# Differential attention on one core: a context projection group moves to another PSUM bank, and in two units of nine the first third of a projection group moves ahead of values and transposes

## The chip, the core and the metric

The kernel runs on one core of a Trainium2 chip. The core has a TensorE for matrix products (PE in the profile, PEld for its weight loads), a VectorE (DVE), a ScalarE (ACT), a GpSimd (POOL) and a SyncE (SP), which issues this kernel's DMAs. Each engine works through its own list of instructions in order and waits on semaphores for the others. Products are written to PSUM, here a tile PS of eight banks with 512 float32 columns each on 128 partitions; only VectorE and ScalarE read it in this kernel.

The metric is the device time of one execution in microseconds. The time before is 2961.78 us, the median of three runs (2960.13 to 2971.89).

## The reference

A two-layer backbone over 1024 latent tokens and 256 context tokens of width 1024. Layer 0 mixes tokens by differential attention, layer 1 by an S5 state space model; both are followed by an MLP. The change lies in the attention of layer 0: eight heads, each with two query/key halves of 64 columns and values of 128.

```python
def attend(q, k, v):
    s = jnp.einsum('bqhcd,bkhcd->bhcqk', q, k).astype(jnp.float32)
    p = jax.nn.softmax(s, axis=-1)
    w = p[:, :, 0] - lam * p[:, :, 1]
    o = jnp.einsum('bhqk,bkhe->bqhe', w.astype(v.dtype), v)
    return rmsnorm(o, subln_g) * (1.0 - lambda_init)
...
k_all = jnp.concatenate([k_c, k_l], axis=1)
o_l = lax.map(lambda qq: attend(qq, k_all, v_all), qb)
...
o_c = attend(q_c, k_c, v_c)
```

Latent queries read all 1280 keys, context queries the 256 context keys.

## The kernel before

Products that need more precision than one pass gives are made as three: each operand is split into a high and a low part (`split`: ScalarE copies the high part, VectorE or GpSimd subtracts), and `mm3` adds high by high, high by low and low by high (lines 132 to 134, so three matmuls stand for one product of 128 rows).

`phase_b` is the attention. For each of eight heads h it goes through nine units u. Unit 0 holds the 256 context queries, units 1 to 8 hold 128 latent queries each. In a unit

- `scores` (L517) multiplies queries by keys. In units 1 to 8 it fills 2560 columns, which are banks 0 to 4 of PSUM: 1280 for each half. In unit 0 it uses half of each of banks 0 to 3; bank 4, the scores' fifth, is then unused.
- `maxima` (L538 for unit 0, L542 for the others) lets VectorE copy the negated scores out with their minimum, one instruction for each half, which frees the banks. `exps` (L549, L552) takes the exponentials on ScalarE, `combine` (L560 to L563) forms the weight difference on VectorE.
- `w_part` (L570, L575) transposes the weights of the unit before in three parts on TensorE, into bank 5, the upper half of bank 6, and bank 7 (or bank 5 again, when the unit has a projection group). `w_evac` empties them: the first part directly (L583 on ScalarE, L584 on VectorE), the others by a ScalarE copy (L588) that GpSimd splits (L589, L590). In units whose values belong to a latent pair, the flag `late` puts all of this behind the exponentials.
- `values` multiplies the transposed weights of a pair of units by the values, into bank 6: 6 matmuls in unit 2, 30 in units 1, 4, 6 and 8, none in units 0, 3, 5 and 7.
- `proj_group` projects part of the next head's keys (T=1) or queries (T=0) for one token group g: 2 is the context (256 columns), 0 and 1 are the latent halves (512 columns). The table AHEAD says which unit makes which:

```python
AHEAD = {0: ((1, 2), (1, 0)), 2: ((1, 1),), 3: ((0, 2),), 5: ((0, 0),), 7: ((0, 1),)}
```

A group is eight products, 24 matmuls, and a list of steps behind it. All groups take their bank from `self.qb`, which in `phase_b` holds bank 7 alone. A context group is evacuated by `direct` (L462 on ScalarE, L463 on VectorE) into the staging tile `stg` and stored to DRAM. A latent group goes through `evac` (L467, L468), a swap of rows by four DMAs, a product with the sine on GpSimd (L473), a sum on VectorE (L476), a split and a store. Unit 0 has two groups: the first is made whole before the scores, the second, like the single group of the other units, in three pieces (`fills`) behind the three parts of the transposes.

On PE, DVE, ACT and POOL the order of `phase_b` is the order in which it is written (`self.manual()`). SyncE's order, and everything outside `phase_b`, is set by a scheduler that plans with its own estimate of times. Key tiles, queries and values are loaded back from DRAM by `load_k`, `load_q` and `load_v`; `load_k(h + 1, 1)` is written in unit 8, since its buffer is that of a key tile which the scores of unit 8 read.

Of the kernel before, what the change touches and what calls it, by code (L numbers as in the profile page):

```python
# [70 lines left out]
class Prog:  # L71
# [64 lines left out]
    def split(self, hi, lo, src, lo_eng=None):  # L136
        self.nc.scalar.activation(hi, src, AF.Copy)  # L137
        (lo_eng or self.nc.vector).tensor_tensor(lo, src, hi.bitcast(F32), ALU.subtract)  # L138
# [302 lines left out]

        return split

    def proj_group(self, h, T, g, wt):

        nc = self.nc
        n, c0 = self.G_TOK[g], (256, 768, 0)[g]
        b = self.qb.next()[:, 0:n]
        scale = 1.0 if T else -0.125
        t = slice(c0 - 256, c0 + 256)  # L450
        hT = self.hT[g]
        q, sw, qc, s = self.rq, self.rs, self.rc, self.stg[:, :, 0:n]

        def product(k):
            return lambda: self.mm3(b, wt[k][0], wt[k][1], hT[0][:, k], hT[1][:, k], k == 0, k == 7)

        def out():
            dst = self.Kd if T else self.Qd
            self.dma(dst[h % 2, :, :, c0 : c0 + n].rearrange("l p n -> p l n"), s.bitcast(F32))

        def direct():
            nc.scalar.activation(s[:, 0], b, AF.Copy, scale=scale)  # L462
            nc.vector.scalar_tensor_tensor(s[:, 1], b, scale, s[:, 0].bitcast(F32), ALU.mult, ALU.subtract)  # L463
            out()

        def evac():
            nc.scalar.activation(q, b, AF.Copy, scale=scale)  # L467
            nc.vector.scalar_tensor_tensor(qc, b, scale, self.cosT[:, t], ALU.mult, ALU.mult)  # L468
            for j in range(4):
                self.dma(sw[32 * j : 32 * j + 32], q[32 * (j ^ 1) : 32 * (j ^ 1) + 32])  # L470

        def sine():
            nc.gpsimd.tensor_tensor(sw, sw, self.sinT[:, t], ALU.mult)  # L473

        def add():
            nc.vector.tensor_tensor(qc, qc, sw, ALU.add)  # L476

        def store():
            self.split(s[:, 0], s[:, 1], qc)
            out()  # L480

        return [product(k) for k in range(8)], [direct] if g == 2 else [evac, None, sine, add, store]
# [143 lines left out]
    def phase_b(self):  # L626
# [14 lines left out]
        def load_k(h, c):  # L641
            K = loaded[h, "k", c] = self.rv(0, 1280) if (h, c) == (7, 1) else Kr.next()
            for k0, k1 in ((0, 256), (256, 1280)):
                self.dma(K[:, k0:k1].bitcast(F32), self.Kd[h % 2, c, :, k0:k1])

        def load_v(h):
            V = loaded[h, "v"] = Vr.next(), Vr.next()
            for j in range(2):
                self.dma(V[j].bitcast(F32), self.Vd[h, j])

        def load_q(h, pair):
            Q = Qr.next()
            cols = slice(256 * pair, 256 * pair + 256)
            self.dma(Q.bitcast(F32), self.Qd[h % 2, :, :, cols].rearrange("l p n -> p l n"))
            loaded[h, pair] = Q

        def values(h, pair):
            V = loaded[h, "v"]
            last = 2 if pair == 0 else 10
            for kt in range(last):  # L660
                self.mm3(pb[:, 0:256], V[0][:, kt], V[1][:, kt], self.wT[0][:, kt], self.wT[1][:, kt],
                         kt == 0, kt == last - 1)
# [107 lines left out]
        def wo_group(i):  # L770
            g = 2 if i > 7 else i // 4
            c0 = 128 * (i - self.G_TILES[g][0])
            b = self.bank(i - 6 if 6 < i < 8 else 7)

            def product(k):
                hh, hl = (t[:, k, c0 : c0 + 128] for t in self.oT[g])
                return lambda: self.mm3(b, hh, hl, wt6[k][0], wt6[k][1], k == 0, k == 5)

            def out():
                wsum = wsums.next()  # L780
                nc.scalar.activation(wsum, b, AF.Copy)
                self.dma(self.wod[i], wsum)

            return [product(k) for k in range(6)], [out]
# [13 lines left out]
        wts = {1: split(1)}  # L798
# [12 lines left out]
        with self.manual():  # L811
            for n in range(72 + 5):
                h, u = units[n] if n < 72 else (8, 9)
                front = n < 72
                groups = []
# [7 lines left out]
                if front:  # L823
                    K = loaded[h, 'k', 0], loaded[h, 'k', 1]
                    pair = (u + 1) // 2
                    Q = loaded[h, pair]
                    s0 = hst[:, 0, h]
                    p, sn, sm = (p0.next(), p1), self.stat.next(), self.stat.next()
                    if u == 5 and h < 7:
                        load_v(h + 1)  # L830
                        load_k(h + 1, 0)
                    if u % 2 == 0 and u < 8 and (h, pair + 1) not in loaded:
                        load_q(h, pair + 1)
                    if h < 7:
                        groups = [self.proj_group(h + 1, *a, wts[a[0]]) for a in self.AHEAD.get(u, ())]
                    if len(groups) == 2:
                        for f in groups[0][0] + groups[0][1]:
                            f()
                    self.scores(u, Q, K)
                    if u == 8 and h < 7:  # L840
                        load_k(h + 1, 1)
                        load_q(h + 1, 0)
                        load_q(h + 1, 1)
                    self.maxima(u, p, sm)
# [6 lines left out]
                if 65 <= n < 75:  # L851
                    groups = [wo_group(wo_order[n - 65])]
                fills = [[], [], []]
                if h >= 7 and groups:
                    fills = [groups[0][0][i : i + 2] for i in (0, 2, 4)]
                elif groups:
                    fills = [groups[-1][0][i:j] for i, j in (((0, 4), (4, 8), (8, 8)) if u == 3 else ((0, 3), (3, 6), (6, 8)))]
                if pv:
                    values(*pv)
                for part in range(3):  # L860
# [1399 lines left out]
```

## Time and profile before

| | before |
|---|---|
| median of the runs | 2961.78 us |
| the profiled execution, its own time | 2967.23 us |
| its span, first to last instruction | 2965.4 us |
| granted TensorE clock over the span | 0.98 |
| attention, first scores of head 0 to the last of head 7 | 227.5 to about 891 us |
| busy in 400 to 500 us: PE, DVE, ACT, POOL | 93.4, 79.6, 56.2, 62.6 us of 100 |

The page has the span and the busy time of each engine, and names lines as `L517`. In an answer on waits, a line gives the engine and line that waited, after the arrow the one that ended the wait, the total in us, how often, and the longest. A row of the timeline gives start and duration in us, the engine, the line, the operation with output and inputs, the shape and a count; in brackets stand the idle time of that engine just before and who ended it. "SPq" is the issue of a DMA, whose transfer comes later. A row of windows gives the stretch, its length, the busy time of PE, PEld, DVE, ACT and POOL, the granted clock as a share of full speed, the share of the DMA engines' time, and GB/s.

### The profile page before, as it was taken

To read this page: it belongs to the slowest core of one execution; us is meant where nothing else is said; L and a number is where in the kernel's file an instruction comes from. 1 tells how busy PE (TensorE), PEld (TensorE's weight loads), DVE (VectorE), ACT (ScalarE), POOL (GpSimd) and SP (SyncE) were. 2 spreads that over 40 slices of the span, in tenths; PEclk is the share of its full clock that TensorE was granted. 3 is DMA by queue.
4 is the path that set the end of the run, shared out by engine and by line. 5 is a ranking of instruction groups with operands and counts; after the bars stand their busy time and mean duration, and the time that the engine had idled before them with its cause. 6 is when DMAs were issued, how large, how long until landed. Compare 5 with 4: busy or idle time off the path is not lost.

```text
span 2965.4 us, 44388 instructions
## 1 busy us (share of the span) xinstructions
PE 2795.9 (94%) x16040; PEld 2315.8 (78%) x16040; DVE 1884.1 (64%) x2777; ACT 1311.9 (44%) x2412; POOL 1010.5 (34%) x911
## 2 busy tenths in 40 slices
PE   6998999999899999999999999969899999999999
PEld 4686878778777787788777778768788778887887
DVE  6356787787764564444487863788733676658566
ACT  3324555555553753333422231347534655334443
POOL 2313576666653600000100000668401323326324
PEclk9999999999999999999999999989999999999999
DMA  9953344444634546422566673468944475467544
GB/s 277 301 188 132 126 154 146 154 144 133 203 124 149 156 127 193 141 94 89 177 189 189 182 232 109 134 193 269 302 134 150 148 228 195 152 201 267 162 137 140
DMA packets 422920, 512.95 MB, mean 173 GB/s; under 512 B 57142, under 2 KB 295980, under 8 KB 421548
## 3 DMA queue, kind: packets, MB, share of 16 engines
q1 hardware_dynamic: 422700, 510.11, 55.2%
q8 instruction: 126, 2.06, 0.3%
q14 instruction: 94, 0.77, 0.1%
HBM read 351.29 MB, written 154.50 MB: 171 GB/s over the span
## 4 chain that ended last, share of the span: by engine, by line
PE 49%; DVE 8%; DMA 5%; issue 5%; POOL 4%; ACT 3%; SPq 2%; DVEq 0%; POOLq 0%; ACTq 0%
PE PS L132 15%; PE PS L133 15%; PE PS L134 15%; SPq L80 2%; PE PS L1722 1%; PE PS L1763 1%; ACT F L552 1%; DVE F L542 1%; DVE FD L1742 1%; DVE H L138 1%; DMA K<-in_mlp_w 1%; PE PS L517 1%; DVE FD L1639 1%; DMA W<-in_mlp_w 1%; DMA H<-hidd 1%
## 5 line engine op out<-in xcount | busy, mean ns | idle before, releaser
L132 PE MATMUL PS<-H,R 128*128 128x512 f32 (+1 forms) x816 | 306.2, 378 | 23.2 <-ACT F L588 15.8
L132 PE MATMUL PS<-H 128*128 128x512 f32 x768 | 300.7, 393 | 2.9 <-ACT H L137 2.9
L134 PE MATMUL PS<-H 128*128 128x512 f32 x768 | 300.2, 392 | 1.9 <-DVE H L138 1.9
L133 PE MATMUL PS<-H 128*128 128x512 f32 x768 | 301.2, 392 | 0.0
L133 PE MATMUL PS<-H,R 128*128 128x512 f32 (+1 forms) x816 | 297.5, 365 | 1.4 <-POOL H L138 1.4
L134 PE MATMUL PS<-H,R 128*128 128x512 f32 (+1 forms) x816 | 297.0, 365 | 0.0
L137 ACT ACTIVATE R<-W 128x512 fp32r<-128x512 f32 (+1 forms) x186 | 132.9, 720 | 194.4 <-PE PS L133 149.5
L132 PE MATMUL PS<-R,H 128*128 128x512 f32 x540 | 216.7, 405 | 1.8 <-ACT R L137 1.6
L552 ACT ACTIVATE F<-F,stat 128x1280 f32<-128x1280 f32 x128 | 174.4, 1363 | 96.1 <-DVE F L542 95.8
L133 PE MATMUL PS<-R,H 128*128 128x512 f32 x540 | 212.1, 394 | 0.0
L134 PE MATMUL PS<-R,H 128*128 128x512 f32 x540 | 210.5, 394 | 1.0 <-DVE H L138 1.0
L138 DVE TENSOR_TENSOR H<-W,H 128x512 fp32r<-128x512 f32 (+1 forms) x145 | 137.0, 953 | 107.1 <-ACT H L137 100.3
L542 DVE TENSOR_SCALAR_CACHE_REDUCE F<-PS 128x1280 f32<-128x1280 f32 x128 | 185.2, 1482 | 23.1 <-PE PS L517 23.1
L132 PEld LDWEIGHTS PS<-H,R 128*128 128x128 f32 x816 | 158.5, 195 | 49.0 <-ACT F L588 17.2
L138 DVE TENSOR_TENSOR R<-W,R 128x512 fp32r<-128x512 f32 (+1 forms) x149 | 125.0, 844 | 104.0 <-ACT R L137 78.3
L589 POOL TENSOR_SCALAR R<-F 128x256 fp32r<-128x256 f32 (+1 forms) x128 | 127.8, 998 | 176.1 <-ACT F L588 154.1
L137 ACT ACTIVATE H<-W 128x512 fp32r<-128x512 f32 (+2 forms) x166 | 107.1, 653 | 177.8 <-PE PS L133 114.6
L134 PEld LDWEIGHTS PS<-H,R 128*128 128x128 f32 x816 | 158.5, 194 | 25.1 <-issue 1.2
L133 PEld LDWEIGHTS PS<-H,R 128*128 128x128 f32 x816 | 159.4, 195 | 22.8 <-POOL H L138 1.6
L517 PE MATMUL PS<-R,R 64*128 64x256 f32 (+1 forms) x1380 | 157.3, 348 | 16.0 <-DVE F L542 6.6
L132 PEld LDWEIGHTS PS<-H 128*128 128x128 f32 x768 | 144.8, 189 | 35.4 <-ACT H L137 3.8
L134 PEld LDWEIGHTS PS<-H 128*128 128x128 f32 x768 | 144.8, 189 | 33.2 <-DVE H L138 2.8
(450 smaller groups left out, 7226.5 us busy)
## 6 DMA issues: line engine op xcount, KB each, us to landing
W<-in_mlp_w SPq DMA_DIRECT2D x192, 256.0 KB
Ad<-F SPq DMA_DIRECT2D x112, 256.0 KB
W<-Ad SPq DMA_DIRECT2D x112, 256.0 KB
W<-in_ada_w SPq DMA_DIRECT2D x32, 512.0 KB
W<-in_mlp_w SPq DMA_DIRECT2D x32, 512.0 KB
H<-hidd SPq DMA_DIRECT2D x64, 256.0 KB
U<-in_ada_w SPq DMA_DIRECT2D x32, 512.0 KB
W<-in_s_w_glu SPq DMA_DIRECT2D x64, 256.0 KB
```

The source lines that it names most:

```text
L80: return self.nc.sync.dma_start(out=out, in_=in_)
L132: mm(out, ah, bh, start=first, stop=False, **kw)
L133: mm(out, ah, bl, start=False, stop=False, **kw)
L134: mm(out, al, bh, start=False, stop=last, **kw)
L137: self.nc.scalar.activation(hi, src, AF.Copy)
L138: (lo_eng or self.nc.vector).tensor_tensor(lo, src, hi.bitcast(F32), ALU.subtract)
L517: mm(self.PS[:, o : o + k1 - k0], Q[rows, i, qs], K[j][rows, k0:k1], start=n == 0, stop=n == 2)
L542: ts(p[c], self.PS[:, 1280 * c : 1280 * c + 1280], 1.0, None, ALU.mult, ALU.min, accum_out=sm[:, c : c + 1])
L552: nc.scalar.activation(p[c], p[c], AF.Exp, bias=sm[:, c : c + 1], scale=-1.0, accum_out=sn[:, 0:1] if c else s0[:, u + 1 : u + 2])
L589: nc.gpsimd.tensor_scalar(hi, t, 1.0, 0.0, ALU.mult, ALU.add)
L1639: v.scalar_tensor_tensor(y, w, r, x, ALU.mult, ALU.add)
L1722: mm(b[:, o : o + 160], X[:, d, i, 64 * j : 64 * j + 128], U[:, 4 * n + i, cols], start=True, stop=True)
```

## The change

Two things are done. In unit 0, the first group, the context's keys of the next head, is given bank 4 instead of bank 7; the second group keeps bank 7. In units 2 and 7 of heads 0 to 6 the first piece of the group, three products or nine matmuls, is made before `values` and the transposes, and the other two pieces move up by one part of the transposes, so that nothing of the group stands behind the third part.

```diff
-    def proj_group(self, h, T, g, wt):
+    def proj_group(self, h, T, g, wt, bank=None):
...
-        b = self.qb.next()[:, 0:n]
+        b = (self.qb.next() if bank is None else bank)[:, 0:n]
...
-                        groups = [self.proj_group(h + 1, *a, wts[a[0]]) for a in self.AHEAD.get(u, ())]
+                        groups = [self.proj_group(h + 1, *a, wts[a[0]], self.bank(4) if u == 0 and i == 0 else None)
+                                  for i, a in enumerate(self.AHEAD.get(u, ()))]
...
                     fills = [groups[-1][0][i:j] for i, j in (((0, 4), (4, 8), (8, 8)) if u == 3 else ((0, 3), (3, 6), (6, 8)))]
+                if h < 7 and u in (2, 7):
+                    for f in fills[0]:
+                        f()
+                    fills = fills[1:] + [[]]
                 if pv:
                     values(*pv)
```

TensorE's list at unit 2 of head 0, from the end of the scores (inputs R_1814 are keys, R_106 alone is weights by values, H the hidden states of a projection, F_1815 the weights to transpose). Before:

```order
L517 MATMUL PS<-R_1814,R_106 128x256 x2
L132 MATMUL PS<-R_106 128x256
L133 MATMUL PS<-R_106 128x256
L134 MATMUL PS<-R_106 128x256
L132 MATMUL PS<-R_106 128x256
L133 MATMUL PS<-R_106 128x256
L134 MATMUL PS<-R_106 128x256
L575 MATMUL PS<-ident,F_1815 128x128 x4
L132 MATMUL PS<-H,R_106 128x512
L133 MATMUL PS<-H,R_106 128x512
L134 MATMUL PS<-H,R_106 128x512
```

The same place now:

```order
L517 MATMUL PS<-R_1814,R_106 128x256 x2
L132 MATMUL PS<-H,R_106 128x512
L133 MATMUL PS<-H,R_106 128x512
L134 MATMUL PS<-H,R_106 128x512
L132 MATMUL PS<-H,R_106 128x512
L133 MATMUL PS<-H,R_106 128x512
L134 MATMUL PS<-H,R_106 128x512
L132 MATMUL PS<-H,R_106 128x512
L133 MATMUL PS<-H,R_106 128x512
L134 MATMUL PS<-H,R_106 128x512
L132 MATMUL PS<-R_106 128x256
```

Nine projection matmuls have moved ahead of the six of the values; in unit 7, which has no values, they have moved ahead of the first four transposes in the same way.

The bank of the first group shows only in what its first matmul waits for: at unit 0 of head 1 it was ScalarE (the copy that empties bank 7) and is now VectorE (the maxima that empty bank 4).

SyncE's list at the turn from head 0 to head 1, where the planner has changed it. FC<-FC are the row swaps, Qd<-R the store of projected queries, R_1814<-Kd the loads of the second key tile of head 1 (256 context columns, 1024 latent ones). Before:

```order
L80 DMA Qd<-R_106 128x2x512
L80 DMA FC<-FC 32x512 x4
L80 DMA R_1814<-Kd 128x256
L80 DMA R_1814<-Kd 128x1024
L80 DMA R_106<-Qd 128x2x256
```

Now:

```order
L80 DMA FC<-FC 32x512 x2
L80 DMA Qd<-R_106 128x2x512
L80 DMA FC<-FC 32x512 x2
L80 DMA R_1814<-Kd 128x256
L80 DMA R_1814<-Kd 128x1024
L80 DMA R_106<-Qd 128x2x256
```

Two of the swaps have moved ahead of the store; the key loads still follow behind all of them.

## The prediction, made before the changed kernel was run

> **What bounds the kernel now.** I read the page first, then TensorE's waits in the attention stage, then the timeline around each wait.
>
> ```profile
> span 2965.4 us, 44388 instructions
> PE 2795.9 (94%) x16040; PEld 2315.8 (78%) x16040; DVE 1884.1 (64%) x2777; ACT 1311.9 (44%) x2412; POOL 1010.5 (34%) x911
> PE PS L132 <- ACT F L588: 15.8, 6, 2.9
> PE PS L575 <- DVE R L584: 13.1, 9, 2.5
> PE PS L132 <- DVE R L463: 6.0, 1, 6.0
> PE PS L133 <- DVE R L584: 5.5, 7, 1.5
> ```
>
> TensorE is busy 94% of the span, so a change to the order of its work can only pay by its waits. The last four lines are those waits between 220 and 900 us (total, times, longest). Each belongs to one place of the head loop. L588 is the copy that empties bank 7 (six times, at unit 0 of heads 1 to 6). L463 is the direct evacuation of a context group from bank 7 (once, head 0). L584 on L133 is unit 2. L584 on L575 is mostly unit 5, which the change doesn't touch, and head 7, which has no projection groups. In unit 7 of heads 0 to 6 TensorE doesn't wait at all.
>
> **The change part by part.** No instruction is added, removed or resized: the same matmuls write the same number of columns. What changes is one bank and the place of nine matmuls in two units of nine.
>
> *Head 0.* The two unit-0 groups share bank 7, so the second waits for the evacuation of the first:
>
> ```profile
> 227.50 1.65 PE L517 MATMUL PS<-R,R 64*128 64x256 f32 x12 [3.88 <-issue]
> 235.13 0.79 PE L132 MATMUL PS<-H,R 128*128 128x512 f32 x1 [5.98 <-DVE R L463]
> 243.59 2.38 PE L517 MATMUL PS<-R,R 64*128 64x256 f32 x21
> 234.24 0.38 ACT L462 ACTIVATE R<-PS 128x256 fp32r<-128x256 f32 x1 [12.81 <-DMA Qd<-R]
> 236.02 0.42 DVE L538 TENSOR_SCALAR_CACHE_REDUCE F<-PS 128x256 f32<-128x256 f32 x1
> ```
>
> That evacuation waited 12.81 us for an earlier store to leave the staging tile. With the first group in bank 4, the second group (24 matmuls, 235.13 to 243.59) starts right behind the scores of unit 0, at 229.2. The next scores then start at 237.6 in place of 243.59: **6.0 us**. Next late are the maxima of unit 0, which leave the banks at 236.4, so no more than 7.1 us can be had; if unit 1 found another wait, 0.
>
> *Unit 0 of heads 1 to 6.* Head 2's boundary:
>
> ```profile
> 384.95 1.48 DVE L542 TENSOR_SCALAR_CACHE_REDUCE F<-PS 128x1280 f32<-128x1280 f32 x1
> 388.31 0.86 ACT L588 ACTIVATE F<-PS 128x256 f32<-128x256 f32 x2
> 389.23 0.39 PE L132 MATMUL PS<-H,R 128*128 128x256 f32 x1 [2.89 <-ACT F L588]
> 392.30 0.98 PE L517 MATMUL PS<-R,R 64*128 64x256 f32 x12
> 386.89 0.86 SPq L80 DMA_DIRECT2D R<-Kd  x2
> 393.27 0.37 SPq L80 DMA_DIRECT2D Kd<-R  x1
> 397.49 0.32 SPq L80 DMA_DIRECT2D R<-Kd  x1
> ```
>
> Bank 4 is free when the second maximum of unit 8 has read it, at 386.4, and TensorE has nothing before 386.3. The 24 matmuls (3.1 us) can thus end at 389.6 instead of 392.3, 2.7 us earlier. **Next late is a DMA**: the scores of unit 0 read the next head's second key tile, whose load SyncE issues at 386.89, behind stores. The trace shows no landing. The nearest row is the 256 KB store at 393.27, on which the load at 397.49 waits: 4.2 us. I take 4.2 us for the 128 KB load too (bounds: 0.9, when both issues are over, and 5.4, the scores' start in the run). The load then lands at 391.1 and the scores gain 1.2 us. The other boundaries:
>
> ```profile
> 306.71 1.08 SPq L80 DMA_DIRECT2D R<-Kd  x2
> 311.46 0.98 PE L517 MATMUL PS<-R,R 64*128 64x256 f32 x12
> 470.43 0.58 PE L132 MATMUL PS<-H,R 128*128 128x256 f32 x1 [2.85 <-ACT F L588]
> 468.09 0.86 SPq L80 DMA_DIRECT2D R<-Kd  x2
> 475.84 1.32 PE L517 MATMUL PS<-R,R 64*128 64x256 f32 x12
> 551.97 0.86 SPq L80 DMA_DIRECT2D R<-Kd  x2
> 558.87 0.97 PE L517 MATMUL PS<-R,R 64*128 64x256 f32 x12
> 634.71 0.85 SPq L80 DMA_DIRECT2D R<-Kd  x2
> 641.61 0.98 PE L517 MATMUL PS<-R,R 64*128 64x256 f32 x12
> 718.23 0.86 SPq L80 DMA_DIRECT2D R<-Kd  x2
> 725.21 1.24 PE L517 MATMUL PS<-R,R 64*128 64x256 f32 x12
> 470.00:476.00 6.00, 5.57 (x26) 5.35 (x26) 2.52 (x3) 1.11 (x4) 5.83 (x6) 0.50 0.95 304
> ```
>
> Scores' start less (issue + 4.2) gives 0.55, 3.55, 2.7, 2.7 and 2.8 us; with head 2's 1.2 **13.5 us**. Heads 3 to 6 gain more because their group runs at half clock after the wait (the last line: granted clock 0.50; the group takes 5.4 us instead of 3.1). The least is 0; the most, if loads and VectorE never bind, is the waits' 15.8 plus 2.3 for each of the four slowed groups, had all been as slow as head 3's: 25.
>
> [...]
>
> *Unit 2.* Nine matmuls (2.2 us) now stand between the scores and the values:
>
> ```profile
> 410.40 0.39 PE L133 MATMUL PS<-R 128*128 128x256 f32 x1 [0.74 <-DVE R L584]
> 419.41 0.69 DVE L468 SCALAR_TENSOR_TENSOR FC<-PS,W 128x512 f32<-128x512 f32 x1
> 420.69 1.49 DVE L542 TENSOR_SCALAR_CACHE_REDUCE F<-PS 128x1280 f32<-128x1280 f32 x1 [0.58 <-PE PS L517]
> ```
>
> They cover the 0.74 us wait. Next late is VectorE, 0.58 us behind it: its maxima of unit 3 waited only that long for TensorE. So at most 0.58 us for each of heads 1 to 6, about 3.4 in all. At least it is nothing, or a loss of 0.4 us a head if ScalarE's copy of the later transposes is pushed as in unit 7.
>
> *Unit 7.* There was no wait to cover, and the transposes come 2.2 us later. ScalarE empties them ahead of the exponentials:
>
> ```profile
> 372.90 0.58 ACT L583 ACTIVATE R<-PS 128x512 fp32r<-128x512 f32 x1
> 373.98 1.37 ACT L552 ACTIVATE F<-F,stat 128x1280 f32<-128x1280 f32 x1 [0.51 <-DVE F L542]
> 376.27 1.75 DVE L476 TENSOR_TENSOR FC<-FC 128x512 f32<-128x512 f32 x1 [0.30 <-POOL FC L473]
> ```
>
> The transposes end near 374.7 now, so the copy moves there from 372.90 and pushes the first exponential from 373.98 to 375.3, 1.3 us. Queued behind it on ScalarE is the second exponential, and VectorE's combine waits for both: two of 1.37 us with their accumulator reads end near 378.4. VectorE's addition, 1.75 us from 376.27, runs until 378.0 and covers all but 0.4 us. In seven heads that is 2.8 us lost; without the cover 9; if a later unit has slack for it, 0. I set units 2 and 7 against each other: 3.4 gained, 2.8 lost, rounded to **0**.
>
> *The rest.* SyncE's order is planned, not written: two of the four row swaps now stand ahead of the query store, but the key loads keep their place. Behind attention the planner also interleaves norm and MLP work differently; no row prices that. The nearest is TensorE's largest wait for work there:
>
> ```profile
> PE PS L1722 <- DVE FD L1733: 17.5, 15, 7.7
> ```
>
> A third of it won or lost by another order is 6 us. I take 0, with 6 either way, since the work and its dependences stay.
>
> Sum: 6.0 + 13.5 + 0 = **19.5 us**. The profiled execution took 2967.23 us, 1.8 us beyond its span, and 5.4 us over the median of the runs, 2961.78. The difference is taken from the median: 2961.78 - 19.5 = **2942 us**.
>
> **The rivals.**
>
> *VectorE binds at unit 0 instead of the load.* For it: ScalarE's first evacuation in unit 0 is in line behind a split that waits for VectorE, and VectorE adds a rotary product that waits for GpSimd:
>
> ```profile
> 391.42 0.42 ACT L137 ACTIVATE W<-W 128x256 fp32r<-128x256 f32 x1 [1.98 <-POOL R L590]
> 395.13 1.15 DVE L476 TENSOR_TENSOR FC<-FC 128x512 f32<-128x512 f32 x1
> 397.09 0.16 DVE L560 RECIPROCAL stat<-stat 128x1 f32<-128x1 f32 x1 [0.81 <-ACT F L549]
> ```
>
> Neither moves with TensorE. The combine of unit 0 can then start at 396.2 at best, 0.9 us earlier. Six boundaries at 1 us and head 0 give 12: 2950 us. Against it: the maxima behind it wait for later products, which do move.
>
> *More than forecast:* loads land sooner and the clock stays up. 7.1 + 20 = 27 us: 2935.
>
> *The change doesn't do what it says:* the second group's bank 7, or the loads, hold TensorE as long as bank 7 did, and head 0's 6.0 us is spent in unit 1. Then it is 2962. Against it: by 392.3 bank 7 has been empty for 3 us.
>
> *Slower:* the key load goes late. It stands behind stores whose data pass VectorE (normalisation), ScalarE and GpSimd, and unit 7 now makes VectorE late. The load decides as soon as it lands after the 392.30 at which scores start today; each microsecond beyond costs 6. With the uncovered 1.3 us through that chain and 4.2 us of contention it lands 2.5 us after: 15 us, 2977. Against it: 1.2 to 3.6 us of slack, and a delay of 0.4.
>
> **How the numbers follow.** Forecast 0.58, VectorE 0.22, more 0.09, no effect 0.05, slower 0.06. The forecast's own range, 6 us about 2942, goes to 2936 and 2948; with VectorE's case above it and part of the larger gain below it, 2933 to 2956 leaves less than 2 in 10 out. 0.5% is 14.8 us, about what a measurement can tell from no change. Faster by that: most of the forecast, all of "more": 0.66; within: VectorE, no effect and the forecast's weak end: 0.27; slower 0.07.
>
> **What would show it.** Right: no wait on L588 ahead of unit 0's 256-column products; unit 0's scores waiting a little for a DMA; no granted clock of half at the boundaries; no 6 us wait at 235; unit 2's wait on L584 gone. VectorE's rival shows in TensorE waits on L542 or L468 in units 1 to 3. The slower rival shows scores of unit 0 waiting for R<-Kd over 3 us. The forecast is wrong if attention ends less than 15 us earlier, or if it does and the rest gives it back.

## The result, and the profile after

| | before | after |
|---|---|---|
| median of the runs | 2962.53 us (6 runs, 2960.13 to 2971.89) | 2947.6 us (6 runs, 2944.5 to 2951.44) |
| the profiled execution's span | 2965.4 us | 2949.7 us |
| attention, first scores of head 0 to the first of head 7's last unit | 227.50 to 888.87 us | 228.35 to 872.83 us |

The ratio, estimated from all runs, is 0.9942 with a 95% interval of 0.9929 to 0.9956. The medians differ by 14.9 us, which is just the 0.5% that the prediction set as its bound. The changed kernel is faster: less so than was forecast (2942), but inside the range.

First the page's two top lines of the changed kernel, then TensorE's waits between 220 and 900 us (engine and line that waited, who ended it, total us, times, longest):

```profile
span 2949.7 us, 44385 instructions
PE 2795.1 (95%) x16040; PEld 2315.4 (78%) x16040; DVE 1877.9 (64%) x2777; ACT 1309.8 (44%) x2412; POOL 1016.2 (34%) x911
...
PE PS L575 <- DVE R L584: 13.8, 9, 3.2
PE PS L517 <- DVE F L542: 7.5, 4, 2.9
PE PS L132 <- DVE FC L468: 5.8, 7, 1.1
PE PS L517 <- DMA R<-Kd: 5.5, 5, 2.0
...
PE PS L517 <- DMA Vd<-R: 3.1, 1, 3.1
...
PE PS L133 <- DVE R L584: 0.6, 1, 0.6
```

The two waits on bank 7, 15.8 us on L588 and 6.0 us on L463, are gone, and so is unit 2's wait on L584 in all heads that were changed (5.5 to 0.6; what is left is head 7's, which has no projection group). TensorE's busy time is the same to a microsecond, so the 15.7 us of the span are time in which it stood idle. Two waits are new: unit 3's group waits seven times for L468 (5.8 us), and unit 0's scores wait five times for the key load (5.5 us). The scores of other units wait 7.5 us for maxima, four times; in head 0 that will matter below.

Where the time went is read best from the length of units: from the first scores matmul of one unit to that of the next. Head 2's unit 0 shows how. These are rows of the timeline of the changed kernel:

```profile
381.20 1.48 DVE L542 TENSOR_SCALAR_CACHE_REDUCE F<-PS 128x1280 f32<-128x1280 f32 x1
382.75 0.38 PE L132 MATMUL PS<-H,R 128*128 128x256 f32 x1 [0.22 <-DVE F L542]
385.81 0.38 PE L517 MATMUL PS<-R,R 64*128 64x256 f32 x2
386.98 0.85 PE L517 MATMUL PS<-R,R 64*128 64x256 f32 x10 [0.79 <-DMA R<-Kd]
395.00 2.38 PE L517 MATMUL PS<-R,R 64*128 64x256 f32 x21
383.13 0.86 SPq L80 DMA_DIRECT2D R<-Kd  x2
```

The group in bank 4 starts 0.2 us behind the maximum that empties it, and the 24 matmuls run without a gap. The scores begin at 385.81, wait 0.79 us for the second key tile, whose load was issued at 383.13, and unit 0 lasts until 395.00, so 9.19 us. The table has these lengths from one profiled execution of each kernel (mean of heads 2 to 6; units 7 and 8 of heads 1 to 5, which include the groups made ahead of the next head's unit 0; units 1 and 2 are taken together):

| us | head 0, units 0 to 3 | unit 0 | 1 and 2 | 3 | 4 | 5 | 7 and 8 | all of attention |
|---|---|---|---|---|---|---|---|---|
| before | 38.76 | 8.25 | 17.85 | 6.91 | 7.20 | 11.18 | 24.30 | 661.4 |
| after | 35.52 | 9.81 | 16.81 | 8.16 | 7.20 | 11.16 | 20.04 | 644.5 |

A head gains 4.3 us in units 7 and 8, up to the next head's scores, and gives 1.6 back in unit 0, where the scores now wait. Unit 2 gains 1.0, and unit 3 loses 1.25. Head 0's first units gain 3.2.

### The profile page after: what moved, and what is told of

It reads as the page before. It is cut to its first block, busy times and chain, and to the rows that moved or that the text cites. A ratio compares the mean times of both kernels' runs of the same rounds, so it can differ in the third digit from the quotient of the medians.

```text
span 2949.7 us, 44385 instructions
## 1 busy us (share of the span) xinstructions
PE 2795.1 (95%) x16040; PEld 2315.4 (78%) x16040; DVE 1877.9 (64%) x2777; ACT 1309.8 (44%) x2412; POOL 1016.2 (34%) x911
## 4 chain that ended last, share of the span: by engine, by line
PE 55%; DVE 6%; DMA 5%; ACT 3%; issue 2%; SPq 2%; POOL 1%; DVEq 0%; POOLq 0%; ACTq 0%
PE PS L132 17%; PE PS L134 17%; PE PS L133 17%; SPq L80 2%; PE PS L1727 1%; DVE FD L1747 1%; DMA U<-in_ada_w 1%; DVE H L138 1%; DMA W<-in_mlp_w 1%; DMA H<-xb 1%; PE PS L204 1%; PE PS L1768 0%; ACT F L552 0%; DMA W<-recd 0%; DVE F L542 0%
## 5 line engine op out<-in xcount | busy, mean ns | idle before, releaser
L132 PE MATMUL PS<-H,R 128*128 128x512 f32 (+1 forms) x816 | 302.9, 374 | 8.3 <-DVE FC L468 5.8
L133 PE MATMUL PS<-H,R 128*128 128x512 f32 (+1 forms) x816 | 293.9, 360 | 1.4 <-POOL H L138 1.4
L134 PE MATMUL PS<-H,R 128*128 128x512 f32 (+1 forms) x816 | 293.8, 361 | 0.0
L542 DVE TENSOR_SCALAR_CACHE_REDUCE F<-PS 128x1280 f32<-128x1280 f32 x128 | 185.1, 1482 | 18.5 <-PE PS L517 18.5
L589 POOL TENSOR_SCALAR R<-F 128x256 fp32r<-128x256 f32 (+1 forms) x128 | 135.8, 1061 | 162.2 <-ACT F L588 144.6
L132 PEld LDWEIGHTS PS<-H,R 128*128 128x128 f32 x816 | 154.9, 190 | 37.2 <-DVE FC L468 7.4
L134 PEld LDWEIGHTS PS<-H,R 128*128 128x128 f32 x816 | 154.7, 190 | 26.4 <-POOL R L138 1.4
L133 PEld LDWEIGHTS PS<-H,R 128*128 128x128 f32 x816 | 155.5, 191 | 22.7 <-POOL H L138 1.7
```

The costliest lines, as they stand in the source:

```text
L132: mm(out, ah, bh, start=first, stop=False, **kw)
L133: mm(out, ah, bl, start=False, stop=False, **kw)
L134: mm(out, al, bh, start=False, stop=last, **kw)
L542: ts(p[c], self.PS[:, 1280 * c : 1280 * c + 1280], 1.0, None, ALU.mult, ALU.min, accum_out=sm[:, c : c + 1])
L589: nc.gpsimd.tensor_scalar(hi, t, 1.0, 0.0, ALU.mult, ALU.add)
```

## The experiments

All times are medians beside runs of the kernel before on the same chip. The last table has the unit lengths of all of them but the first try with four key buffers. They come from one profiled execution each, and single boundaries differ by up to two microseconds between executions of one kernel (compare the two of the changed kernel), so only what shows in every head or in several runs is read from them.

**The bank alone.** The pieces stay where they were:

```diff
-                if h < 7 and u in (2, 7):
+                if h < 7 and u in ():
```

> The bank alone, groups of units 2 and 7 in the old order. Theory A (the bank makes the gain; in unit 2 the covered wait comes back one unit later as a wait on VectorE's L468): attention ends 15 to 16.5 us earlier than before, ratio 0.994 to 0.996; unit 2 keeps its waits of 0.75 us on L584, and unit 3 has none on L468. Theory B (the early pieces carry a good part): attention ends 8 to 12 us earlier, ratio 0.996 to 0.998.

2945.15 us, ratio 0.9940 (0.9924 to 0.9957): the whole gain. TensorE's waits in attention with the bank alone:

```profile
PE PS L575 <- DVE R L584: 13.2, 9, 2.5
PE PS L517 <- DMA R<-Kd: 8.2, 5, 2.6
...
PE PS L133 <- DVE R L584: 5.8, 7, 1.5
```

Unit 2's wait on L584 is back, and no wait on L468 appears. Units 1 and 2 are longer than in the changed kernel by 1.1 us and unit 3 is shorter by 1.25: the piece in unit 2 only moves the wait. Units 7 and 8 take 20.03 us against 20.04: the piece in unit 7 neither costs nor gains anything. In head 0, units 0 to 3 take 33.18 us with the bank alone, and 34.4 to 35.8 in the six profiles that have the bank and the piece behind unit 2's scores: 1.3 to 2.6 us more, 2.3 in the profile of after. Of that, 1.35 is unit 3 (6.90 with the bank alone, 8.25 to 8.27 in the six), where the group waits for L468 as in the other heads; only this part can be put down to the piece, as the section on the prediction shows.

**The pieces alone.** Both context groups stay in bank 7:

```diff
-                        groups = [self.proj_group(h + 1, *a, wts[a[0]], self.bank(4) if u == 0 and i == 0 else None)
+                        groups = [self.proj_group(h + 1, *a, wts[a[0]], None)
```

> The early pieces in units 2 and 7 alone, both groups of unit 0 in bank 7. Theory A: the waits of unit 2 on L584 go, unit 3 gets waits on L468 of the same size or VectorE is no earlier, the waits of 2.9 us on L588 and of 6 us on L463 stay; attention ends within 2 us of before, ratio 0.999 to 1.001. Theory B: 4 to 8 us earlier, ratio 0.997 to 0.9985.

2968.87 us, ratio 1.0013 (1.0002 to 1.0024): no gain. The waits with the pieces alone have both of the old ones, and L468's:

```profile
PE PS L132 <- ACT F L588: 16.7, 6, 3.0
...
PE PS L132 <- DVE R L463: 6.3, 1, 6.3
PE PS L132 <- DVE FC L468: 4.5, 7, 0.9
```

**The key load taken off the boundary, first try.** A fourth buffer for key tiles, and `load_k(h + 1, 1)` in unit 5 instead of 8. In this version head 7's second key tile still goes to its old place, `rv(0, 1280)`, which in unit 5 of head 6 still holds weights of head 7's queries; so part of head 7's query projection is computed from other data, and TensorE waits 7.5 us there for the load.

> The changed kernel with a fourth key buffer, so that the second key tile of the next head is loaded in unit 5 instead of unit 8. If the key load binds at unit 0: the five waits on R<-Kd (5.5 us in all) go, half clock at head 5 (627.9 to 631.4 us) doesn't come, and attention ends 4 to 7 us earlier than with the change. If VectorE binds there: the scores of unit 0 start earlier, but unit 4 of each head starts within 0.5 us of the changed kernel's shift, except for about 3 us at head 5 from the clock; 2 to 3.5 us in all.

2961.28 us, ratio 0.9995 (0.9985 to 1.0005); unit 5 of head 6 takes 20.8 us instead of 11.2, so the total tells nothing. Up to unit 4 of head 6, ahead of that wait, attention had gained 17.08 us on the kernel before, the changed kernel 17.12. That is a first sign that the load alone isn't what holds the boundary.

**The same, with the fourth buffer for head 7 too:**

```diff
-        Kr = Ring([self.view(self.R1, 5 * i, (1280,)) for i in range(3)])
+        Kr = Ring([self.view(self.R1, 5 * i, (1280,)) for i in (0, 1, 2, 4)])
...
-            K = loaded[h, "k", c] = self.rv(0, 1280) if (h, c) == (7, 1) else Kr.next()
+            K = loaded[h, "k", c] = Kr.next()
...
                         load_k(h + 1, 0)
+                        load_k(h + 1, 1)
...
-                        load_k(h + 1, 1)
```

> The changed kernel with a fourth buffer for key tiles, into which the next head's second key tile is loaded in unit 5 (5 KB more of SBUF), so that unit 0's scores have no late load to wait for. Theory L (the key load is what is next late at unit 0, as the prediction has it): the waits of unit 0's scores on R<-Kd, 5.5 us in 5, go, and with them the half clock behind the longest, 3.4 us: 6 to 9 us less than the changed kernel's 2947.6, so 2939 to 2942. Theory V (VectorE and ScalarE's line in unit 0 is late right behind the load, and the maxima come no sooner): TensorE then waits on the maxima, L542, in units 1 and 2 instead, over 12 us in all heads against 7.5 in the changed kernel, and the time stays within 2 us of it: 2945.5 to 2949.5.

2952.95 us, ratio 0.9955 (0.9943 to 0.9968): not faster than the changed kernel (0.9942), though no scores of unit 0 wait for a load any more. TensorE's waits, and a row of head 3's unit 2:

```profile
PE PS L575 <- DVE R L584: 15.5, 13, 2.5
PE PS L517 <- DVE F L542: 15.1, 9, 4.2
PE PS L132 <- DVE FC L468: 6.8, 7, 1.1
```

```profile
482.97 2.39 PE L517 MATMUL PS<-R,R 64*128 64x256 f32 x21 [0.94 <-DVE F L542]
```

Unit 0 is 1.5 us shorter (8.30 for 9.81) and units 1 and 2 are 1.7 us longer (18.51 for 16.81): the scores of unit 2 now wait for maxima, about 1 us in each of heads 2 to 6 (the other four waits on L542 are in heads 0 and 7, where the changed kernel has them too). Units 0 to 2 together take 26.8 us against 26.6. Theory V is right on this point: the load is late, but VectorE is just as late behind it.

**The normalisation moved too.** Three of the five normalisations of the head before go from the ends of units 8, 0 and 1 to those of units 1, 2 and 3, beside the four key buffers:

```diff
+        NORM = {6: 0, 7: 1, 1: 2, 2: 3, 3: 4}
...
-                if h < 8 and n - 6 >= 9 and (n - 6) % 9 < 5 and (n - 6) // 9 < 7:
-                    norm_pair((n - 6) // 9 - 1, (n - 6) % 9)
+                if 15 <= n < 69 and u in NORM:
+                    norm_pair((n - 6) // 9 - 1, NORM[u])
```

> As the kernel with four key buffers, and three of the five normalisations of the head before (a VectorE product of 0.5 to 0.7 us, L700, and a split on ScalarE and GpSimd, L137 and L590) go from the ends of units 8, 0 and 1 to those of units 1, 2 and 3. Theory V with its reason (at unit 0 the first evacuation L462 stands on ScalarE behind the split's L137, which waits 2 us for GpSimd, and VectorE's line between the maxima of units 0 and 1 is full): L462 comes 1 to 2 us earlier, TensorE's waits on L542 fall by 4 us or more, and the kernel is 4 to 10 us faster than the one with four key buffers alone. Rival (the exponentials and the combine hold the line, not the normalisation): within 2 us of it.

2951.99 us, ratio 0.9949 (0.9936 to 0.9961): no faster. But the lengths show that the reason was right and its consequence wrong. In heads 2 to 6 L462 starts 0.2 us behind the start of unit 0's scores instead of 2.2 to 2.8, units 1 and 2 fall from 18.51 to 16.74 us, and unit 2's scores no longer wait. Units 3, 4 and 5 take 1.7 us more instead. Rows of head 3's unit 5:

```profile
509.59 2.38 PE L517 MATMUL PS<-R,R 64*128 64x256 f32 x21 [1.14 <-DVE F L542]
513.72 0.66 PE L575 MATMUL PS<-ident,F 128*128 128x128 f32 x4 [1.75 <-DVE R L584]
```

The waits on L542 fall only from 15.1 to 13.9 us in all: what was late behind the old place is late three units further on. Which of the moved instructions counts (VectorE's product, ScalarE's copy or GpSimd's subtraction) isn't separated by this run. The two waits on VectorE are ahead of unit 5's scores and of its transposes; in the changed kernel the first isn't there and the second is 1.45 us.

**The piece in unit 5, where the wait is, and in unit 2:**

```diff
-                if h < 7 and u in (2, 7):
+                if h < 7 and u in (2, 5):
```

> The bank, and the early piece in units 2 and 5 instead of 2 and 7. Unit 5 waits 1.45 us on L584 in each of heads 1 to 6, unit 7 doesn't wait. If TensorE's waits are what costs: up to 8.7 us less than the changed kernel. If VectorE sets the pace there (L584 itself is late): the wait goes from unit 5 and comes back behind it; 0 to 2 us less.

2946.88 us, ratio 0.9948 (0.9934 to 0.9963). The waits in this kernel:

```profile
PE PS L132 <- DVE FC L468: 5.0, 7, 1.1
PE PS L575 <- DVE R L584: 4.4, 3, 2.5
```

Unit 5's wait is covered (13.2 in 9 to 4.4 in 3; the three are in head 7), and unit 5 is 0.7 us shorter in each head, with nothing given back in units 6 to 8. The total doesn't show it (ratio 0.9948, the changed kernel's 0.9942), and in this profile unit 0 is 1.1 us longer (10.87 for 9.81): its scores wait 1.7 to 2.3 us for the key load in heads 4 to 6, each time with half clock behind (1.6 to 1.7 us more than 8.30 and the wait), where the changed kernel's profile has that in one head (0.51, behind 1.99 us). In the next run, with the piece in unit 5 too, unit 0 takes 10.10. Unit 2's piece again only makes the waits on L468.

**The piece in unit 5 alone** (`u in (5,)`):

> The bank as in the changed kernel, and the early products in unit 5 instead of units 2 and 7. Theory A' (early products pay only where TensorE waits for transposes with VectorE ahead of its work, which is unit 5, and in unit 2 they only turn the wait on L584 into one on L468 in unit 3): the waits of transposes on L584, L575's line, fall from 13.8 us in 9 to under 5, no wait on L468 appears, L133's wait on L584 in unit 2 is back (5.8 in 7), and attention ends 17 to 20 us before that of the kernel before, 1 to 4 us sooner than in the changed kernel: 2943 to 2946. Rival (unit 5's gain is taken back behind it as unit 2's was): attention ends as with the bank alone, 15.7 us sooner than before, and unit 6 or 7 shows a new wait as large as the old one.

2942.49 us, ratio 0.9919 (0.9907 to 0.9932). Its waits:

```profile
PE PS L133 <- DVE R L584: 6.0, 7, 1.5
PE PS L575 <- DVE R L584: 5.0, 3, 3.1
```

No wait on L468 is left, and that on L584 in unit 2 is back. Attention takes 638.0 us, 6.5 less than in the profile of the changed kernel and 3.4 less than in its second one (at the end of this section). 1.3 to 2.4 us of that are head 0's first units (33.10), where unit 2 has no piece; 4.4 are unit 5's 0.7 us in heads 1 to 6, and head 7 and single boundaries differ by some tenths to two microseconds either way.

**Head 0's piece ahead of the scores.** The changed kernel, but in unit 2 of head 0 the nine matmuls fill the wait ahead of the scores:

```diff
+                    if (h, u) == (0, 2):
+                        for f in groups[0][0][0:3]:
+                            f()
                     self.scores(u, Q, K)
```

> The changed kernel, but in unit 2 of head 0 alone the nine early products stand ahead of that unit's scores, where TensorE waits 2.87 us for the maxima of unit 1, instead of behind them. Theory C (that wait, and the half clock it brings from 242 to 249, is where head 0's 6.0 us of the forecast became 3.2): no half clock there, head 0 ends 2 to 2.7 us earlier than in the changed kernel, and the time is some 2 us less, 2945 to 2946. Rival (VectorE's own line in units 2 and 3 sets head 0, and TensorE's clock does not matter): head 0 ends within 0.5 us of the changed kernel.

2945.56 us, ratio 0.9926 (0.9915 to 0.9938). Head 0's first four units take 31.53 us, 4.0 less than the changed kernel's 35.52 (2.9 less than in its second profile) and 7.2 less than the kernel before: more than expected. The timeline, and the windows behind it (granted clock in the seventh figure, 1.00):

```profile
240.61 0.50 PE L132 MATMUL PS<-H,R 128*128 128x512 f32 x1
243.43 2.38 PE L517 MATMUL PS<-R,R 64*128 64x256 f32 x21 [0.48 <-DVE F L542]
247.02 0.66 PE L575 MATMUL PS<-ident,F 128*128 128x128 f32 x4 [0.30 <-DVE F L563]
```

```profile
240.00:249.00 9.00, 8.08 (x51) 6.20 (x51) 7.95 (x12) 4.71 (x7) 2.37 (x2) 1.00 0.23 60
```

**The two gains together:** the piece in unit 5, and head 0's ahead of unit 2's scores.

> The bank, the early products in unit 5 instead of units 2 and 7, and in unit 2 of head 0 alone nine products ahead of the scores. If the two gains add up, units 0 to 3 of head 0 take 31.5 us as in the run with the cover and not 33.1 as with the early products in unit 5 alone, and the time is 1 to 2 us under that run's 2942.5: 2941. If head 0's gain is lost by the first head boundary, 2942.5 or more.

2943.99 us, ratio 0.9933 (0.9918 to 0.9948). In attention the two add up: head 0's units 0 to 3 take 31.52 us, and all of it 634.4 us, 3.6 less than with the piece in unit 5 alone; 1.6 of that are head 0's, the rest are single boundaries. The median doesn't show it: it is 1.5 us longer than that of the run with the piece in unit 5 alone, on another chip, and runs of this one kernel differ by 10 us (2937.11 to 2947.42).

**All moves:** to this, the four key buffers and the moved normalisation.

> As the run with early products in unit 5 and the cover in head 0, with four key buffers and the normalisation in units 1, 2, 3 added. Theory V (load, normalisation and the wait for transposes in unit 5 stand one behind the other, so each alone gains nothing and all together gain): from head 2 on unit 0 takes 8.3 us instead of 9.2 to 11.7, units 1 and 2 at most 6.6 and 11.3, unit 5's wait stays under 1.5 us, and the kernel is 4 to 9 us faster than that run: 2932 to 2937. Rival (VectorE's work of a head is the bound, and where it stands does not matter): units 3 to 5 grow by what units 0 to 2 lose, and the time is within 2 us of that run.

2941.06 us, ratio 0.9924 (0.9911 to 0.9938). Rows of TensorE's timeline in head 2:

```profile
399.98 0.39 PE L133 MATMUL PS<-R 128*128 128x256 f32 x1 [0.52 <-DVE R L584]
423.18 2.38 PE L517 MATMUL PS<-R,R 64*128 64x256 f32 x21 [1.15 <-DVE F L542]
```

For attention the rival is right: unit 0 is 1.9 us shorter than in the run before it, unit 4 is 1.2 and unit 5 0.3 longer, and attention as a whole takes 633.75 us against 634.4. The medians differ by 2.9 us, less than the 4 to 9 of theory V, and the intervals of the two overlap.

**The changed kernel once more**, on the chip of the last two:

> The changed kernel once more, on the same chip as the two others, so that they can be compared with it: 2945 to 2950.

2947.2 us, ratio 0.9941 (0.9928 to 0.9953). The three versions with the piece in unit 5 and none behind unit 2's scores are 1 to 2 tenths of a per cent better than it by their ratios; the intervals overlap. In attention they are 3 to 11 us shorter than its two profiles (641.4 and 644.5); for the whole time that isn't settled.

| us | head 0, units 0 to 3 | unit 0 | 1 and 2 | 3 | 4 | 5 | 7 and 8 | all of attention |
|---|---|---|---|---|---|---|---|---|
| the bank alone | 33.18 | 10.66 | 17.94 | 6.91 | 7.19 | 11.17 | 20.03 | 644.5 |
| the pieces alone | 39.77 | 8.19 | 16.75 | 7.92 | 7.19 | 11.19 | 24.44 | 662.7 |
| four key buffers, second try | 35.75 | 8.30 | 18.51 | 8.37 | 7.20 | 11.18 | 20.04 | 647.0 |
| and the normalisation moved | 34.47 | 8.30 | 16.74 | 8.53 | 8.41 | 11.47 | 20.04 | 645.7 |
| pieces in units 2 and 5 | 34.56 | 10.87 | 16.75 | 8.01 | 7.19 | 10.44 | 20.04 | 643.1 |
| piece in unit 5 | 33.10 | 10.10 | 17.95 | 6.91 | 7.19 | 10.43 | 20.03 | 638.0 |
| head 0's piece ahead | 31.53 | 9.85 | 16.77 | 8.08 | 7.19 | 11.17 | 20.04 | 641.6 |
| piece in unit 5, head 0's ahead | 31.52 | 10.17 | 17.74 | 6.91 | 7.19 | 10.44 | 20.03 | 634.4 |
| all moves | 31.51 | 8.30 | 17.62 | 6.91 | 8.41 | 10.74 | 20.05 | 633.8 |
| the changed kernel again | 34.44 | 10.01 | 16.75 | 7.93 | 7.19 | 11.19 | 20.04 | 641.4 |

## Why the prediction was right, and where it wasn't

The sum was 19.5 us, and the span lost 15.7. From the profiles, attention starts 0.85 us later (over all the kernels here it starts between 227.4 and 230.9 us, so that is chance), head 0 gains 3.2, the six boundaries with the units between them gain 13.9, head 7 loses 0.2, and the rest of the program 0.4.

*Head 0: the term that was mis-sized,* 6.0 us in the forecast and 3.2 in the run. Its mechanism held: the 6 us wait on L463 is gone, and the scores of unit 1 start 7.9 us sooner (after the start of attention; only their first matmul, the others wait 0.31 us more for the maxima of unit 0). The forecast asked whether unit 1 would find another wait, and priced none. The wait came in unit 2, on the maxima of unit 1. It was there before, with 2.42 us, and the gain made it longer. The timeline of the changed kernel shows what stands behind it:

```profile
237.23 2.38 PE L517 MATMUL PS<-R,R 64*128 64x256 f32 x20 [0.31 <-DVE F L538]
243.25 4.03 PE L517 MATMUL PS<-R,R 64*128 64x256 f32 x21 [2.87 <-DVE F L542]
259.52 0.39 PE L132 MATMUL PS<-H,R 128*128 128x256 f32 x1 [0.94 <-DVE FC L468]
```

```profile
242.20:249.10 6.90, 5.76 (x26) 4.61 (x27) 5.31 (x9) 2.52 (x4) 1.28 (x1) 0.51 0.13 27
```

Behind the wait of 2.87 us the clock is at half (0.51) for 6.9 us, and the scores take 4.03 us, where unit 1's took 2.38. The unit lengths of head 0 in the runs above take clock and order apart:

| us, head 0 | units 0 and 1 | unit 2 | unit 3 | half clock at unit 2 | gain in all |
|---|---|---|---|---|---|
| before | 21.47 | 10.37 | 6.92 | none | |
| after | 14.90 | 12.35 | 8.27 | 6.8 | 3.2 |
| the changed kernel again | 14.93 | 11.26 | 8.25 | 3.4 | 4.3 |
| the bank alone | 14.94 | 11.34 | 6.90 | 3.4 | 5.6 |
| piece in unit 5 | 14.91 | 11.27 | 6.91 | 3.4 | 5.7 |
| head 0's piece ahead | 14.98 | 8.30 | 8.26 | none | 7.2 |

Units 0 and 1 gain 6.5 to 6.6 us in every run with the bank, which is the forecast's 6.0 and a little more. Unit 2 loses about 1 us where half clock lasts 3.4 us, whether or not the piece stands behind its scores, and 2 us in the profile of after, where it lasted twice as long. Unit 3 loses 1.35 us whenever nine matmuls of unit 2's group are early, by the wait on L468 (the term of unit 2, below). So the size of 3.2 is partly chance: a second execution of the same kernel gained 4.3. With the piece ahead of the scores the wait is 0.48 us and the clock stays up (1.00 from 240 to 249). That head 0's 7.2 us there is close to the 7.1 that the forecast had named as the most is chance too, since 2.1 of it come from the wait in unit 2, which the forecast did not count, and 1.35 are lost again in unit 3.

In the profile of after, the clock was at half for the first 3.41 us of attention (0.50 from 228.58) and at full from there on, so that unit 1's scores, behind the 24 matmuls, took 2.38 us. Behind the single wait of 2.87 us it was at half again (0.50 from 242.23 to 249.06).

*The boundaries: right in size, 13.5 us forecast and 13.9 measured,* and bank 4 is what makes it (with the pieces alone the six lose 0.8 us together). One by one they are 1.4, 1.4, 4.0, 2.6, 0.6 and 3.9 against 0.6, 1.2, 3.6, 2.7, 2.7 and 2.8. The one that falls short is head 5:

```profile
622.87 0.86 SPq L80 DMA_DIRECT2D R<-Kd  x2
627.92 1.44 PE L517 MATMUL PS<-R,R 64*128 64x256 f32 x10 [1.99 <-DMA R<-Kd]
```

```profile
627.90:631.40 3.50, 3.48 (x17) 3.05 (x18) 2.13 (x10) 1.65 (x5) 3.50 (x4) 0.51 1.09 349
```

The load took 5.1 us from its issue instead of 4.2 (in head 2 it took 3.9, from 383.13 to 386.98), and the wait of 1.99 us brought half clock, while the forecast expected none at the boundaries. The close match of the sum is partly luck: in the second profile of the changed kernel the six gain 14.3 us, and head 4 is the one that falls short (0.9: a wait of 1.56 us, and half clock behind it, with products of 0.63 us instead of 0.39); with the bank alone, where two boundaries ran into half clock (one of them, with 0.81 over 9 us, is shown in the last section), they gain 10.5.

*What is next late at unit 0* was named as the key load alone, and that was half of it. The load is waited for, as forecast, five times. But taking it away gains nothing, because VectorE, the rival with 22%, stands at most a few tenths behind it. So the rival's mechanism is there, without its price: at unit 0 it binds only once the load is gone. The sign that the forecast had named for it, waits on L468 or L542 in units 1 to 3, did appear in the changed kernel, but for other reasons: L468's come from the piece in unit 2, since with the bank alone there are none, and L542's in head 0 was there before.

*Unit 2: 3.4 us forecast, nothing measured.* The wait on L584 was covered as forecast. The step that failed is the "at most 0.58 us" that VectorE was to leave. It took the maxima of unit 3 as VectorE's next concern and left out L468, quoted in the row above them, which reads bank 7 behind the combine. Rows of head 2 in the changed kernel:

```profile
412.23 1.55 DVE L563 SCALAR_TENSOR_TENSOR F<-F,stat 128x1280 f32<-128x1280 f32 x1
414.91 0.69 DVE L468 SCALAR_TENSOR_TENSOR FC<-PS,W 128x512 f32<-128x512 f32 x1
415.65 0.39 PE L132 MATMUL PS<-H,R 128*128 128x256 f32 x1 [0.93 <-DVE FC L468]
```

Unit 3's group writes the same bank 7, so it waits until VectorE has come that far, and VectorE doesn't come sooner: in heads 2 to 6 its maxima of unit 3 start 13.7 to 14.4 us behind the start of unit 2's scores with the piece and 13.7 to 13.9 with the bank alone, though the scores of unit 3 start at 10.2 to 10.5 us instead of 11.3 to 11.5. Without the bank it is the same: with the pieces alone units 1 to 3 of heads 2 to 6 take 24.67 us on average, before 24.76.

*Unit 7: 2.8 us lost in the forecast, none in the run.* Units 7 and 8 take 20.04 us with the pieces and 20.03 with the bank alone. The exponentials of head 1's unit 7 were late, as forecast (371.39, where 373.98 less the 3.75 us gained up to there is 370.2), but no scores waited for it; the forecast had that as a bound. That units 2 and 7 came to 0 together was right, with both terms too large.

*The rest:* 0.4 us lost, inside the 6 either way.

*A sum that doesn't come out.* The rival "slower" has the load land 2.5 us late. By head 2's rows, 1.3 and 4.2 us behind 391.1 are 4.3 us behind 392.30, so its price would have been nearer 26 us than 15. No run went that way.

## What to carry over

When a wait on a buffer goes, look for the next late thing twice: the one that follows at once, and the engine that will be waited for when that one is gone too; here a key load and VectorE stood within a few tenths of a microsecond. Moving independent matmuls ahead paid where TensorE waited and no later unit gave the gain back (unit 5), or gave back less than was gained (ahead of head 0's scores); it only moved the wait where the next user of their bank waits for the same slow engine (unit 2). Compare unit lengths between kernels rather than totals of waits: they show at once what is given back, and where. Take a second profile before explaining one head's length by the change.

## What was not expected of the hardware

Short waits can bring half clock, and not always. With the bank alone, two boundaries of one execution:

```profile
545.87 0.85 PE L517 MATMUL PS<-R,R 64*128 64x256 f32 x10 [1.78 <-DMA R<-Kd]
626.12 0.85 PE L517 MATMUL PS<-R,R 64*128 64x256 f32 x10 [1.49 <-DMA R<-Kd]
```

```profile
543.00:551.00 8.00, 6.22 (x41) 5.08 (x40) 6.14 (x16) 4.23 (x14) 7.35 (x9) 1.00 0.93 300
623.00:632.00 9.00, 7.51 (x43) 6.05 (x42) 6.31 (x15) 3.94 (x13) 6.87 (x8) 0.81 0.94 287
```

The wait of 1.78 us left the clock at full (1.00), the shorter one of 1.49 us did not (0.81 over 9 us): that unit 0 took 11.43 us, 1.6 more than the 8.30 of an unhindered one and its wait. The changed kernel's first profile has full clock behind waits of 0.51, 0.79, 0.88 and 1.35 us and half clock behind 1.99 us (0.51); its second has half clock behind 1.56 us (products of 0.63 us instead of 0.39); with the piece in unit 5 it is full behind 1.63 us (1.00 from 463 to 467) and half behind 1.73 us (0.79 from 543 to 551). Counted over all the profiles here, of the waits of unit 0's scores for the key load none of 1.48 us or less brought half clock (20 of them), all five of 1.90 us and more did, and of the ten between five did. Each of these ten times unit 0 took 1.6 to 1.7 us more than 8.30 and the wait, so boundaries of the same kernel differ by that from one execution to the next.

So in these runs the length of the wait alone doesn't decide. What the traces show besides is how long half clock lasts and where it starts. Two windows of the kernel before and one of the changed kernel:

```profile
469.80:476.60 6.80, 6.17 (x30) 5.95 (x32) 2.96 (x4) 1.65 (x5) 6.46 (x7) 0.50 0.88 274
555.20:558.60 3.40, 3.40 (x18) 3.40 (x18) 1.00 (x2) 0.42 (x1) 3.23 (x5) 0.51 1.02 340
```

```profile
228.60:232.00 3.40, 3.40 (x17) 2.75 (x16) 0.00 (x0) 0.00 (x0) 0.00 (x0) 0.50 1.02 419
```

By the granted clock in the two traces, attention ahead of head 7 has half clock for 13.65, 6.83, 3.41, 3.41 and 6.83 us in the kernel before (from 227.47, 469.82, 555.15, 637.07 and 718.99) and for 3.41, 6.83 and 3.41 us in the profile of after (from 228.58, 242.23 and 627.94): 3.41 us or a whole multiple, and within each execution the starts are whole multiples of it apart. In steps of 3.41 us from these starts (from 5 us behind the first scores), six at full clock were followed by one at half. TensorE was idle for 2.24, 2.58, 2.87 and 2.10 us of the four before and for 1.85 and 1.99 us of the two after, going by the ends of matmuls as the profile models them; no other step at full clock in these two profiles had more than 1.56 us. In the kernel before, head 3's wait of 2.85 us lay with 2.24 us in one step, and half clock came; head 2's of 2.89 us lay across two, with 1.56 and 1.33, and it didn't. With the bank alone, if steps are counted from the half clock behind the wait of 1.49 us (by the products of 0.63 us it ends near 630.9, an estimate), that wait lay in one step and the one of 1.78 us across two, with about 1.4 us in the first. That the idle time of a step decides is the author's estimate from these numbers, and no run tested it.

VectorE is busy 65.6 us of the 79.8 us of head 2 (82%), and TensorE 75.7:

```profile
385.81:411.75 25.94, 24.98 (x171) 21.02 (x170) 20.96 (x38) 14.34 (x32) 16.73 (x18) 1.00 0.72 235
411.75:465.61 53.86, 50.75 (x387) 44.16 (x386) 44.63 (x64) 32.77 (x64) 38.43 (x35) 1.00 0.37 111
```

With an order that is fixed on both engines, 18% of slack was not enough to make room for the normalisation's products (0.5 to 1.6 us, median 0.7) and splits: they hold up TensorE at the ends of units 8, 0 and 1, and at those of units 1, 2 and 3, the one other place tried. Whether some other place has room stays open.
